# Running log-sum-exp over time: three rows per partition, the exponent written over the input, later rows added in PSUM by VectorE

## The chip, the cores and the metric

The kernel runs on one core of a Trainium2 chip. A core has TensorE (PE, matrix products into the PSUM memory), VectorE (DVE), ScalarE (ACT, here for Exp and Ln), GpSimd (POOL), and SyncE (SP), which here issues every transfer between the device memory and the on-chip memory (SBUF). Sixteen DMA engines carry the transfers out. The engines run side by side, each takes its own instructions in order, and they wait for each other by semaphores. The metric is the device time of one execution in microseconds (us), as the median of nine runs.

## What is computed

```python
def reference(x):                      # x: 4 x 4096 x 4128, float32
    out[:, 0, :] = x[:, 0, :].copy()
    for t in range(1, S):
        mx = np.maximum(out[:, t - 1, :], x[:, t, :])
        out[:, t, :] = mx + np.log(np.exp(out[:, t - 1, :] - mx) + np.exp(x[:, t, :] - mx))
```

For each of 4 batches and 4128 columns this is the logarithm of the running sum of exp(x) over 4096 time steps. Input and output are 270.5 MB each.

## The kernel before

A batch is cut in steps of 256 consecutive time steps, 16 steps to a batch, 64 in all. In a step each of 128 partitions holds R = 2 consecutive time steps of all 4128 columns, so that a partition's part of the transfer is one run of 33,024 bytes. One load (L102) brings the step into the tile `xt`; one store (L153) takes it out from the same tile after the results have been written over the input.

The columns are cut in four chunks of 1024 (`CH`), and the last chunk also has a tail of 32. For a chunk, ScalarE writes Exp of both rows as fp16 into a buffer of its own, `et` (L111). TensorE then sums over the partitions with triangular 0/1 matrices: `incl` times the first row adds, for partition p, the first rows of partitions 0 to p; `excl` times the second row adds the second rows of partitions 0 to p-1; `pick` times the carry adds what all earlier steps of the batch came to. All go into one PSUM tile `pt` (L86), which then holds the sums for the first row. ScalarE takes Ln of it into `xt` (L126). After that, two more matmuls with the identity `ident` add the second row, and a second Ln writes the second row of the result. The tail has a small PSUM tile of its own, `qt`, with both rows by matmuls, and one Ln (L149).

The carry is the last partition's sum after the last row. VectorE copies 32 partitions of `pt` to fp16 (L90) and writes what the copy lost as a second fp16 value (L91), two instructions of 1024 columns for each chunk (the function `keep`). The next step's `pick` adds both.

The order of the work is written out by hand, and each engine's queue follows it. Within a step, the method `run` starts a chunk's Exp and first matmuls (`head`) before the Lns of the chunk before it. There are five `xt` buffers, four `et` buffers, three `pt` tiles of two PSUM banks and two `qt` tiles. Loads are issued three steps ahead: before the work of step i comes the load of step i+3, after it the store of step i. Both go to SP's one queue, so a load that waits for its buffer holds the store behind it.

Of the kernel before, what the change touches and what calls it, by code (L numbers as in the profile page):

```python
# [7 lines left out]
FP32 = mybir.dt.float32  # L8
FP16 = mybir.dt.float16
ACT = mybir.ActivationFunctionType  # L10
P = 128
R = 2
CH = 1024
MM = 512
HI, LO = 96, 32


def _constants(nc, pool):


    def tri(base, name):
        t = pool.tile([P, P], FP16, name=name)
        nc.gpsimd.memset(t, 1.0)

        nc.gpsimd.affine_select(
            out=t, in_=t, pattern=[[1, P]], compare_op=mybir.AluOpType.is_ge,
            fill=0.0, base=base, channel_multiplier=-1,
        )
        return t

    def ones_where_zero(bases, step, name):
        t = pool.tile([P, P], FP16, name=name)
        nc.gpsimd.memset(t, 0.0)
        for base in bases:
            nc.gpsimd.affine_select(  # L35
                out=t, in_=t, pattern=[[step, P]], compare_op=mybir.AluOpType.not_equal,
                fill=1.0, base=base, channel_multiplier=1,
            )
        return t

    return (
        tri(0, "incl"),
        tri(-1, "excl"),
        ones_where_zero([0], -1, "ident"),
        ones_where_zero([-(HI + 31), -(LO + 31)], 0, "pick"),
    )


@with_exitstack
def kernel(  # L50
    ctx: ExitStack,
    tc: tile.TileContext,
    x: bass.AP,
    out: bass.AP,
):

    nc = tc.nc
    B, S, D = x.shape  # L60
    rows = P * R
    n_t = S // rows
    assert S % rows == 0
    n_main = D // CH
    tail = D - n_main * CH
    t0 = n_main * CH

    nc.scalar.preload_act_table_set("natural_log_exp_and_others")  # L68
    consts = ctx.enter_context(tc.tile_pool(name="consts", bufs=1))
    incl, excl, ident, pick = _constants(nc, consts)  # L70

    xpool = ctx.enter_context(tc.tile_pool(name="xpool", bufs=5))
    epool = ctx.enter_context(tc.tile_pool(name="epool", bufs=4))
    cpool = ctx.enter_context(tc.tile_pool(name="cpool", bufs=1))
    pmain = ctx.enter_context(tc.tile_pool(name="pmain", bufs=3, space=bass.MemoryType.PSUM))
    ptail = ctx.enter_context(tc.tile_pool(name="ptail", bufs=2, space=bass.MemoryType.PSUM))

    carry = [cpool.tile([P, CH], FP16, name=f"carry{c}") for c in range(n_main)]
    carry_t = cpool.tile([P, tail], FP16, name="carry_t")
    for t in (*carry, carry_t):  # L80
        nc.vector.memset(t, 0.0)  # L81

    ctx.enter_context(tc.manual_schedule())

    def mm(pt, w, rhs, start, stop):
        nc.tensor.matmul(pt, lhsT=w, rhs=rhs, start=start, stop=stop, skip_group_check=True)  # L86

    def keep(cr, pt):

        nc.vector.tensor_copy(cr[HI:HI + 32, :], pt[HI:HI + 32])  # L90
        nc.vector.tensor_tensor(  # L91
            out=cr[LO:LO + 32, :], in0=pt[HI:HI + 32], in1=cr[HI:HI + 32, :],
            op=mybir.AluOpType.subtract,
        )

    class Step:
        def __init__(self, b, k):
            self.first = k == 0
            self.xt = xpool.tile([P, R, D], FP32, name="xt")
            self.et, self.pt = {}, {}  # L100
            self.dram = lambda t: t[b, k * rows:(k + 1) * rows, :].rearrange("(p j) d -> p j d", j=R)
            nc.sync.dma_start(out=self.xt, in_=self.dram(x))  # L102

        def cols(self, c):
            return slice(c * CH, (c + 1) * CH if c + 1 < n_main else D)

        def exp(self, c):
            s = self.cols(c)
            w = s.stop - s.start
            et = epool.tile([P, R, CH + tail], FP16, name="et")  # L110
            nc.scalar.activation(et[:, :, :w], self.xt[:, :, s], ACT.Exp)  # L111
            self.et[c] = et

        def head(self, c):
            et = self.et[c]
            pt = self.pt[c] = pmain.tile([P, CH], FP32, name="pt")
            for s in range(0, CH, MM):
                mm(pt[:, s:s + MM], incl, et[:, 0, s:s + MM], True, False)
            for s in range(0, CH, MM):
                mm(pt[:, s:s + MM], excl, et[:, 1, s:s + MM], False, self.first)  # L120
            if not self.first:
                for s in range(0, CH, MM):
                    mm(pt[:, s:s + MM], pick, carry[c][:, s:s + MM], False, True)

        def ln(self, j, c):
            nc.scalar.activation(self.xt[:, j, c * CH:(c + 1) * CH], self.pt[c], ACT.Ln)  # L126

        def second(self, c):
            pt = self.pt[c]
            for s in range(0, CH, MM):  # L130
                mm(pt[:, s:s + MM], ident, self.et[c][:, 1, s:s + MM], False, True)

        def close(self, c):

            self.ln(1, c)
            keep(carry[c], self.pt[c])

        def tail_mm(self):
            et = self.et[n_main - 1]
            qt = self.qt = ptail.tile([P, R, tail], FP32, name="qt")  # L140
            e0, e1 = et[:, 0, CH:], et[:, 1, CH:]
            for j in range(R):
                mm(qt[:, j, :], incl, e0, j == 0, False)
                mm(qt[:, j, :], incl if j else excl, e1, False, self.first)
                if not self.first:
                    mm(qt[:, j, :], pick, carry_t, False, True)

        def ln_tail(self):
            nc.scalar.activation(self.xt[:, :, t0:D], self.qt, ACT.Ln)  # L149
            keep(carry_t, self.qt[:, 1, :])  # L150

        def store(self):
            nc.sync.dma_start(out=self.dram(out), in_=self.xt)  # L153

        def run(self):
            last = n_main - 1
            self.exp(0)
            self.head(0)
            for c in range(1, n_main):
                self.exp(c)  # L160
                self.head(c)
                if c == last:
                    self.tail_mm()
                self.ln(0, c - 1)
                self.second(c - 1)
                if c >= 2:
                    self.close(c - 2)
            self.ln(0, last)
            self.second(last)
            self.close(last - 1)  # L170
            self.ln_tail()
            self.close(last)
            self.store()

    work = [(b, k) for b in range(B) for k in range(n_t)]
    ahead = 3
    steps = []
    for i, (b, k) in enumerate(work):
        if i == 0:
            steps += [Step(*work[n]) for n in range(ahead)]  # L180
        if i + ahead < len(work):
            n = i + ahead
            steps.append(Step(*work[n]))
        steps[i].run()


# [28 lines left out]
```

The softmax here doesn't subtract the row's maximum and nothing guards it: scores larger than these inputs give would overflow.

## Time and profile before

| what | value |
|---|---|
| median of nine runs | 1265.33 us (1264.34 to 1266.58) |
| the profiled execution: time | 1265.88 us |
| the profiled execution: span from first to last instruction | 1264.1 us |
| busy: ScalarE, TensorE (matmuls), VectorE | 962.7, 665.7, 655.7 us |
| mean granted TensorE clock | 0.764 of full |
| transfers | 64 loads and 64 stores of 4128 KB each |
| from issue to landing, median: loads, stores | 29.4, 38.9 us |
| moved over the span | 541.51 MB, 428 GB/s |

An engine's busy time is the sum of its instructions, and says little about what the end waits for: ScalarE is busy for 76% of the span and is still not what the others wait for most of the time. For that one reads the waits of each engine, and for the transfers the forty slices of the span, in each of which the page gives the share that the DMA engines were busy in tenths, and the GB/s that they moved. A group's line has the engine, the operation, what it writes and reads, the count, then the busy sum and the mean in ns of one, then the idle time just before and what ended it.

### The profile page before, as it was taken

The page shows a single profiled execution, that of the slowest core. Times are in us where ns is not written, and L with a number is a line of the kernel's source. Part 1 is how long each engine was busy: PE and PEld are TensorE (multiplying, and loading weights), DVE is VectorE, ACT ScalarE, POOL GpSimd, SP SyncE. Part 2 cuts the span into 40 slices and gives each one's busy share as a digit, 9 for nine tenths or more (in the row PEclk, how much of TensorE's full clock was granted, in tenths as well). Part 3 has the DMA queues.
Part 4 walks back from the last instruction along what each step waited for, and adds up shares of the span by engine and source line. Part 5 has one row for each costly group of instructions (what it writes and reads, how often), then busy time and mean ns, then how long its engine had stood idle before and what let it go on. Part 6 is the DMA issues. An engine that isn't in the chain of part 4 may idle for free.

```text
span 1264.1 us, 7025 instructions
## 1 busy us (share of the span) xinstructions
PE 665.7 (53%) x2392; PEld 242.8 (19%) x2392; DVE 655.7 (52%) x645; ACT 962.7 (76%) x833; POOL 2.2 (0%) x13
## 2 busy tenths in 40 slices
PE   2666655545455464454554555556545555555551
PEld 1222221212111121121111211112111121112210
DVE  3665654464554645545546455464554544645443
ACT  5988877778677777787877777777778787787872
POOL 0000000000000000000000000000000000000000
PEclk9777777777777777877877777767777777777876
DMA  9999999999999999999999999999999999999997
GB/s 401 420 429 432 433 431 429 430 432 432 431 433 432 433 434 434 434 433 430 434 432 432 432 433 432 434 434 433 433 429 435 433 433 431 431 434 433 434 434 318
DMA packets 18466, 541.51 MB, mean 428 GB/s; under 512 B 2048, under 2 KB 2048, under 8 KB 2048
## 3 DMA queue, kind: packets, MB, share of 16 engines
q1 hardware_dynamic: 18432, 541.07, 99.4%
q8 instruction: 19, 0.31, 0.1%
q14 instruction: 15, 0.12, 0.0%
HBM read 270.53 MB, written 270.53 MB: 428 GB/s over the span
## 4 chain that ended last, share of the span: by engine, by line
DMA 84%; ACT 2%; issue 1%; SPq 1%; DVE 1%; PE 0%; ACTq 0%
DMA out_dram<-xt 80%; DMA xt<-in_x_dram 5%; ACT et L111 1%; ACT xt L126 1%; SPq L102 1%; PE pt L86 0%; DVE carry L90 0%; DVE carry L91 0%; SPq L153 0%; DVE carry_t L90 0%; DVE carry_t L91 0%; ACTq L126 0%
## 5 line engine op out<-in xcount | busy, mean ns | idle before, releaser
L90 DVE CAST carry<-pt 32x1024 f16<-32x1024 f32 x256 | 314.8, 1230 | 576.3 <-ACT xt L126 573.1
L111 ACT ACTIVATE et<-xt 128x2048 f16<-128x2048 f32 (+1 forms) x256 | 485.4, 1920 | 151.9 <-DMA xt<-in_x_dram 151.9
L126 ACT ACTIVATE xt<-pt 128x1024 f32<-128x1024 f32 x512 | 504.5, 1028 | 126.3 <-PE pt L86 65.7
L86 PE MATMUL pt<-et,incl 128*128 128x512 f16 x512 | 211.8, 506 | 548.2 <-ACT et L111 376.5
L91 DVE TENSOR_TENSOR carry<-pt,carry 32x1024 f16<-32x1024 f32 x256 | 314.0, 1227 | 8.8
L86 PE MATMUL pt<-et,excl 128*128 128x512 f16 x512 | 211.9, 506 | 0.0
L86 PEld LDWEIGHTS <-incl 128*128 128x128 f16 x704 | 69.3, 111 | 683.8 <-issue 635.1
L86 PE MATMUL pt<-carry,pick 128*128 128x512 f16 x480 | 195.2, 498 | 0.0
L86 PE MATMUL pt<-et,ident 128*128 128x512 f16 x512 | 175.4, 429 | 26.5 <-ACT xt L126 26.5
L86 PEld LDWEIGHTS <-excl 128*128 128x128 f16 x576 | 71.4, 124 | 116.8 <-issue 85.0
L86 PEld LDWEIGHTS <-pick 128*128 128x128 f16 x600 | 69.5, 118 | 95.1 <-issue 67.2
L86 PEld LDWEIGHTS <-ident 128*128 128x128 f16 x512 | 49.6, 106 | 101.3 <-issue 75.1
L86 PE MATMUL qt<-et,incl 128*128 128x32 f16 x192 | 19.8, 190 | 0.0
L86 PE MATMUL qt<-carry_t,pick 128*128 128x32 f16 x120 | 15.6, 182 | 0.0
L149 ACT ACTIVATE xt<-qt 128x64 f32<-128x64 f32 x64 | 14.5, 227 | 0.0
L90 DVE CAST carry_t<-qt 32x32 f16<-32x32 f32 x64 | 12.6, 197 | 2.0
L91 DVE TENSOR_TENSOR carry_t<-qt,carry_t 32x32 f16<-32x32 f32 x64 | 12.4, 193 | 2.2
L86 PE MATMUL qt<-et,excl 128*128 128x32 f16 x64 | 11.7, 183 | 0.0
L81 DVE MEMSET carry<- 128x512 uint32 x4 | 1.9, 485 | 1.1 <-PEq L199 1.0
L68 ACT ACT_TABLE_LOAD x1 | 1.3, 1283 | 0.8 <-PEq L199 0.8
L35 POOL TENSOR_SCALAR_AFFINE_SELECT pick<-pick 128x128 f16<-128x128 f16 x2 | 0.6, 297 | 0.1
L35 POOL TENSOR_SCALAR_AFFINE_SELECT ident<-ident 128x128 f16<-128x128 f16 x1 | 0.3, 298 | 0.0
(11 smaller groups left out, 1.9 us busy)
## 6 DMA issues: line engine op xcount, KB each, us to landing
xt<-in_x_dram SPq DMA_DIRECT2D x64, 4128.0 KB, 29.4
out_dram<-xt SPq DMA_DIRECT2D x64, 4128.0 KB, 38.9
```

What stands on the lines that cost most here:

```text
L35: nc.gpsimd.affine_select(out=t, in_=t, pattern=[[step, P]], compare_op=mybir.AluOpType.not_equal, fill=1.0, base=base, channel_multiplier=1,)
L68: nc.scalar.preload_act_table_set("natural_log_exp_and_others")
L81: nc.vector.memset(t, 0.0)
L86: nc.tensor.matmul(pt, lhsT=w, rhs=rhs, start=start, stop=stop, skip_group_check=True)
L90: nc.vector.tensor_copy(cr[HI:HI + 32, :], pt[HI:HI + 32])
L91: nc.vector.tensor_tensor(out=cr[LO:LO + 32, :], in0=pt[HI:HI + 32], in1=cr[HI:HI + 32, :], op=mybir.AluOpType.subtract,)
L102: nc.sync.dma_start(out=self.xt, in_=self.dram(x))
L111: nc.scalar.activation(et[:, :, :w], self.xt[:, :, s], ACT.Exp)
L126: nc.scalar.activation(self.xt[:, j, c * CH:(c + 1) * CH], self.pt[c], ACT.Ln)
L149: nc.scalar.activation(self.xt[:, :, t0:D], self.qt, ACT.Ln)
```

## The change

A partition now holds R = 3 consecutive time steps, one run of 49,536 bytes. 4096 is 32 times 128 rows, so a batch has ten steps of three rows and one of two; the two-row step is the last of a batch, and in the first batch the first. There are 44 steps. The `xt` buffers become four of 49.5 KB per partition. Exp is written as fp16 over the first half of the bytes that its chunk of `xt` had, in each row, and the `et` buffers are gone.

A chunk's `head` now puts only the first row's sums into `pt`: `incl` for the first row, `excl` for the second and third, and `pick`. After Ln has read `pt`, VectorE adds the next row's exponents to `pt` in place (`next_row`), and a further Ln follows, and so again for the third row. The identity matrix and its matmuls are gone. In the tail, the second and third row are made by VectorE adds too.

The order in a step runs over g, with the Lns of up to three chunks at different rows in each g. The keeps of chunks that are finished come ahead of the adds as long as a head of this step is still to come, and after the adds and after the last of the step otherwise. SP's order is now store n, then load n+3, both issued after the last Ln of step n.

The core of the diff, the rest of it being the removed class methods and the calls that go with them:

```diff
-R = 2
+R = 3
-    xpool = ctx.enter_context(tc.tile_pool(name="xpool", bufs=5))
-    epool = ctx.enter_context(tc.tile_pool(name="epool", bufs=4))
+    bufs = 4
+    xpool = ctx.enter_context(tc.tile_pool(name="xpool", bufs=bufs))
...
+    def add(o, a, v):
+        nc.vector.tensor_tensor(out=o, in0=a, in1=v, op=mybir.AluOpType.add)
...
-        def exp(self, c):
-            s = self.cols(c)
-            w = s.stop - s.start
-            et = epool.tile([P, R, CH + tail], FP16, name="et")
-            nc.scalar.activation(et[:, :, :w], self.xt[:, :, s], ACT.Exp)
-            self.et[c] = et
...
-        def second(self, c):
-            pt = self.pt[c]
-            for s in range(0, CH, MM):
-                mm(pt[:, s:s + MM], ident, self.et[c][:, 1, s:s + MM], False, True)
...
+        def load(self):
+            full = xpool.tile([P, R, D], FP32, name="xt")
+            self.xt = full[:, :self.r, :]
+            self.half = self.xt.bitcast(FP16)
             nc.sync.dma_start(out=self.xt, in_=self.dram(x))
...
+        def e(self, j, a, b):
+            return self.t.half[:, j, 2 * self.c * CH + a:2 * self.c * CH + b]
+
+        def exp(self):
+            c0, w = self.c * CH, self.w
+            nc.scalar.activation(
+                self.t.half[:, :, 2 * c0:2 * c0 + w], self.t.xt[:, :, c0:c0 + w], ACT.Exp,
+            )
+
+        def head(self):
+            t = self.t
+            pt = self.pt = pmain.tile([P, CH], FP32, name="pt")
+            for j in range(t.r):
+                for s in range(0, CH, MM):
+                    mm(pt[:, s:s + MM], excl if j else incl, self.e(j, s, s + MM), start=j == 0)
+            if not t.first:
+                for s in range(0, CH, MM):
+                    mm(pt[:, s:s + MM], pick, carry[self.c][:, s:s + MM])
+            if self.c == last:
+                self.tail_head()
+
+        def tail_head(self):
+            t, r = self.t, self.t.r
+            full = ptail.tile([P, R, tail], FP32, name="qt")
+            qt = self.qt = full[:, :r, :]
+            e = [self.e(i, CH, CH + tail) for i in range(r)]
+            for i in range(r):
+                mm(qt[:, 0, :], excl if i else incl, e[i], start=i == 0)
+            if not t.first:
+                mm(qt[:, 0, :], pick, carry_t)
+            for i in range(1, r):
+                add(qt[:, i, :], qt[:, i - 1, :], e[i])
+
+        def stage(self, j):
+            t, c = self.t, self.c
+            nc.scalar.activation(t.xt[:, j, c * CH:(c + 1) * CH], self.pt, ACT.Ln)
+            if c == last and j == 0:
+                nc.scalar.activation(t.xt[:, :, t0:D], self.qt, ACT.Ln)
+
+        def next_row(self, j):
+            add(self.pt, self.pt, self.e(j + 1, 0, CH))
...
+    for n, s in enumerate(steps):
+        chunks = [Chunk(s, c) for c in range(n_main)]
+        chunks[0].exp()
+        chunks[1].exp()
+        chunks[0].head()
+        done = []
+        for g in range(n_main + s.r - 1):
+            at = [(chunks[g - d], d) for d in range(s.r - 1, -1, -1) if 0 <= g - d < n_main]
+            for k, d in at:
+                k.stage(d)
+            if g == n_main + s.r - 2:
+                s.store()
+                if n + ahead < len(steps):
+                    steps[n + ahead].load()
+            done += [k for k, d in at if d + 1 == s.r]
+            if g + 1 < n_main:
+                while done:
+                    done.pop(0).keep()
+            for k, d in at:
+                if d + 1 < s.r:
+                    k.next_row(d)
+            if g + 2 < n_main:
+                chunks[g + 2].exp()
+            if g + 1 < n_main:
+                chunks[g + 1].head()
+        for k in done:
+            k.keep()
```

## The prediction

> **What bounds the kernel now.** I read the forty slices first, then the queues, the queue engine's own waits, its timeline, and last the groups of instructions.
>
> ```profile
> DMA  9999999999999999999999999999999999999997
> GB/s 401 420 429 432 433 431 429 430 432 432 431 433 432 433 434 434 434 433 430 434 432 432 432 433 432 434 434 433 433 429 435 433 433 431 431 434 433 434 434 318
> q1 hardware_dynamic: 18432, 541.07, 99.4%
> ```
>
> Every slice but the last has the DMA engines busy, at 429 to 435 GB/s from the third on. 99.4% of the 1264.1 us span, 1256.5 us, is packets of the loads and stores. The kernel is bound by its transfers, and the only slack is some 3 us in the first two slices and 8 us in the last.
>
> ```profile
> SPq L102 <- DMA out_dram<-xt: 1087.8, 59, 19.8
> SPq L153 <- ACT xt L126: 84.5, 7, 17.9
> 566.59 0.33 SPq L102 DMA_DIRECT2D xt<-in_x_dram  x1
> 567.01 0.38 SPq L153 DMA_DIRECT2D out_dram<-xt  x1
> 586.10 0.33 SPq L102 DMA_DIRECT2D xt<-in_x_dram  x1
> 605.60 0.33 SPq L102 DMA_DIRECT2D xt<-in_x_dram  x1
> ```
>
> The first two lines are SP's waits (total, count, longest): 59 of 64 loads wait for an older store to leave its buffer, and only 7 stores wait for ScalarE. The issues come every 19.5 us, and a store goes 0.42 us behind a load because it stood ready and was only queued after it. So a step of 2 rows (8.454 MB both ways) costs 19.5 us of DMA, and a step of 3 rows at this rate 29.3 us.
>
> ```profile
> 29.11 0.34 SPq L153 DMA_DIRECT2D out_dram<-xt  x1
> 45.29 0.34 SPq L153 DMA_DIRECT2D out_dram<-xt  x1
> 61.80 0.34 SPq L153 DMA_DIRECT2D out_dram<-xt  x1
> 78.30 0.34 SPq L153 DMA_DIRECT2D out_dram<-xt  x1
> ```
>
> Near the start the stores do wait for the compute, and show its own pace: 16.2, 16.5 and 16.5 us a step. The compute has 3 us to spare in 19.5. What this change does to that pace decides the case.
>
> ```profile
> L90 DVE CAST carry<-pt 32x1024 f16<-32x1024 f32 x256 | 314.8, 1230 | 576.3 <-ACT xt L126 573.1
> L111 ACT ACTIVATE et<-xt 128x2048 f16<-128x2048 f32 (+1 forms) x256 | 485.4, 1920 | 151.9 <-DMA xt<-in_x_dram 151.9
> L126 ACT ACTIVATE xt<-pt 128x1024 f32<-128x1024 f32 x512 | 504.5, 1028 | 126.3 <-PE pt L86 65.7
> L91 DVE TENSOR_TENSOR carry<-pt,carry 32x1024 f16<-32x1024 f32 x256 | 314.0, 1227 | 8.8
> 617.27 1.01 PE L86 MATMUL pt<-et,incl 128*128 128x512 f16 x2 [5.14 <-ACT et L111]
> 618.08 1.06 PE L86 MATMUL pt<-et,excl 128*128 128x512 f16 x2
> 603.44 0.59 PE L86 MATMUL pt<-et,incl 128*128 128x512 f16 x2 [0.64 <-ACT et L111]
> 603.87 0.59 PE L86 MATMUL pt<-et,excl 128*128 128x512 f16 x2
> ```
>
> These are the durations I use. The matmul pairs show two paces: after 5.14 us of idling a pair follows every 0.81 to 0.85 us, in a busy stretch every 0.43.
>
> **What the Trainium skill says.** "DMA: Bandwidth & Descriptors", Where 436 GB/s comes from: the SBUF ports cap the sixteen engines at about 435 GB/s. The slices agree, at 429 to 435, so longer runs have under 1% to win. The same page, How a descriptor splits into AXI transactions: a start off a 256-byte boundary costs extra beats. 33,024 bytes is 129 times 256, and 49,536 is 193.5 times, so every second partition's run would start off it. No trace here shows that; by the page it is 4 of some 1,550 beats. "VectorE: DVE Perf Modes", The perf-mode tier table: a tensor_tensor with a PSUM operand has only the slowest mode; L91's 1227 ns for 1024 elements agrees. "TensorE: Matmul & The Clock Gate", Part 1: after an idle window of about 3.4 us the array runs at half clock. The two paces above agree.
>
> **The change, part by part.** Loads and stores: 128 of 4128 KB become 80 of 6192 KB and 8 of 4128 KB, the same bytes. A 33 KB packet takes an engine 1256.5/1024 = 1.227 us; at 435 GB/s it would be 1.215. If that 12 ns is per packet, the 320 packets fewer per engine (1024 to 704) save at most 3.8 us; if the excess goes with the bytes, or half is lost to the unaligned starts, 0 to 2 us. I take 2.
>
> SP: before, load i+3 went ahead of store i. Now store n is queued first and load n+3 behind it, so a late compute also holds the load. In flight when store n-1 lands are load n+2, store n and then load n+3, each 14.7 us: 44 us of work, as deep as the 39 us that a store takes to land now. The loads land two steps early, so the order itself costs nothing while the compute keeps pace.
>
> The mask constant, the second matmuls (L86 with ident, 175.4 us of PE) and the separate exponent buffers go. PE is not on the path, so this gains nothing; but PE is now emptier and colder.
>
> New on VectorE: 336 adds of 128x1024 in PSUM (per 3-row step 8, per 2-row step 4). None is in the trace. L91 reads PSUM and SBUF and takes 1.227; I take 1.23 plus the 0.03 seen between VectorE instructions. At best 1.17; at worst, if reading and writing one PSUM bank halves the rate, 2.3. The keeps fall from 256 to 176, and carry_t's from 64 to 44. VectorE's sum is 336 x 1.23 + 176 x 2.46 + 44 x 0.39 + 84 x 0.2, some 880 us of the span. That is no bound by itself, but the add stands between two Lns of one chunk, where a matmul stood before.
>
> ScalarE: Ln goes from 1.028 at 1024 elements to 0.227 at 64, 0.834 ns per element; so an Exp of 3 x 1024 is 1.90 + 0.85 = 2.76, and of 3 x 1056 2.85. A step has 4 Exps, 12 Lns and a tail Ln of 0.25: 23.7 us of work for 29.3 us of DMA. Because Exp writes over x, an Exp and the Ln behind it wait for the end of the one before, which loses the 0.10 us by which neighbours overlap now.
>
> I lay a 3-row step out by hand, with time from Exp of chunk 0, a head of eight matmuls at half clock (8 x 0.43 + 0.16 = 3.6), and 0.03 to 0.1 us for each handover:
> - Exp 0 to 2.8, Exp 1 to 5.55. Head 0 runs 2.8 to 6.4, so Ln of chunk 0 (first row) ends at 7.5; one microsecond is lost to the cold head.
> - Exp 2 to 10.1, two Lns to 12.1, Exp 3 to 14.85, three Lns to 17.7. The adds lie beside the Exps.
> - The keep of chunk 0 is ahead of the adds here, since head 3 needs its PSUM buffer (three buffers, four chunks): VectorE 15.9 to 18.4, then adds of chunks 1 and 2 to 19.7 and 20.95. ScalarE idles from 17.7 to 19.7.
> - Ln chunk 1 (last row) to 20.7, Ln chunk 2 to 22.0. Head 3 runs 18.5 to 22.1, Ln chunk 3 to 23.1, tail Ln to 23.3.
> - Nothing covers the rest: adds of 2 and 3 to 24.55 and 25.8, Lns to 25.6 and 26.85, add to 28.1, last Ln to 29.2. The next Exp starts at 29.1, as neighbours overlap. The remaining keeps lie under the next step's two Exps.
>
> At full clock heads 0 and 3 are 1.7 us shorter each and the period is 27.9, the keep and adds setting the middle. Head 0 follows some 9 us of idle PE and head 3 some 5, so both should be cold: I take 29.0. A 2-row step laid out so comes to 22 against 19.5 of DMA.
>
> The sum on the compute: first load landed at 13.1 (as now), 21 for the first 2-row step, 40 x 29.0, 3 x 22, and 11 for the last store: 1271 us of span. The sum on the DMA: 1264.1 less 2, 1262. The longer one sets the end. The profiled run took 1265.88 with its span 1264.1, and the median of nine is 1265.33, so 1.2 goes on top: **1272 us**.
>
> **The rivals.** A, the compute chain takes the bound, as worked out: 1266 to 1292 for a period of 28.85 to 29.5, likeliest 1272. For it: ScalarE's idle stretches are all dependencies. Against it: its margin over the DMA is 9 us in 1271, 0.25 us a step.
>
> B, on the other side: the DMA keeps the bound and only the packet saving is seen. It decides where the period is under (1262 - 13.1 - 21 - 66 - 11)/40 = 28.8. For it: PEclk 0.76 in the trace, so heads are not always cold, and 27.9 at full clock. Then 1261 to 1262.7, faster, if most of the 12 ns is per packet (1264.1 - 3.8 + 1.2 at best); 1263 to 1265.3, no change, if it isn't.
>
> C, one cost is mis-taken in the large: an add at 2.3 us puts five times 1.07 us on the chain, 40 x 5.3 = 214, near 1485; an add of 1.30 only 14 us, 1286; unaligned runs that cost more than the page's beats come to 12 us for each per cent.
>
> That the change does not do what it says: the bytes are fixed and the runs are contiguous per partition, so they will be 49.5 KB; I give it nothing.
>
> **How the numbers follow.** A 0.60, B faster 0.16, B unchanged 0.16, C 0.08. A measurement of this kernel tells about 0.2%, 2.5 us, from no change. Of A, 0.04 falls within that, so slower is 0.64, same 0.20, faster 0.16. The range takes in B, with 1 us below its best, from 1260, and A with an add or handover somewhat dearer, to 1292; beyond lies most of C. A's own range is 1266 to 1292.
>
> **What would show it.** Right: SP's stores waiting for ScalarE's Ln in most steps at a period of 28.8 to 29.5, DMA slices below 9 or GB/s under 430 late in the run, ScalarE idle behind VectorE's adds, PEclk below 0.76. Wrong: loads still waiting for old stores all along and a cadence of 29.3 with ScalarE waiting for loads (B), or an add far from 1.23 us (C).

## The result and the profile after

The changed kernel takes 1273.48 us (median of nine runs, 1272.98 to 1274.32). The ratio to the kernel before, measured beside it, is 1.0063, with a 95% interval of 1.0055 to 1.0071: 8 us slower. The profiled execution has a span of 1272.1 us against 1264.1.

The slices of the changed kernel (busy tenths, granted clock in tenths, GB/s; each slice is 31.8 us):

```profile
PEclk8666676767667667676666767676666767676666
DMA  9999999999999999999999999999999999999977
GB/s 407 427 429 426 431 435 429 438 429 434 431 436 432 427 438 430 430 441 432 428 434 436 429 435 435 430 439 426 434 435 437 429 435 433 434 435 430 431 312 307
```

The transfers are still full until the last two slices. What is new is there: two slices at 312 and 307 GB/s where the kernel before had one at 318. The DMA engines have work as long as loads run ahead, and when the last load is in they can only wait for stores that come at the pace of the compute. PEclk has gone from 0.764 to 0.674.

SP's waits and its last issues in the changed kernel say who is late:

```profile
SPq L117 <- ACT xt L160: 1201.7, 44, 28.5
SPq L114 <- DMA out_dram<-xt: 6.9, 6, 2.5
1150.64 0.34 SPq L117 DMA_DIRECT2D out_dram<-xt  x1
1179.64 0.34 SPq L117 DMA_DIRECT2D out_dram<-xt  x1
1208.76 51.74 SPq L117 DMA_DIRECT2D out_dram<-xt  x3
```

All 44 stores wait for ScalarE's last Ln, 1201.7 us in total, where before 59 loads had waited 1087.8 us for old stores. Now six loads do, for 6.9 us. The stores come 29.0 to 29.1 us apart, and the last three are spread over 51.7 us because the steps behind them are still being computed.

The chain of waits that ended last (shares of the span by engine), then the waits of ScalarE for a load and for VectorE's adds, and those of the adds for the tail's Ln (L162):

```profile
ACT 48%; DVE 25%; PE 21%; issue 4%; DMA 1%; ACTq 0%
ACT xt L129 <- DMA xt<-in_x_dram: 10.9, 1, 10.9
ACT xt L160 <- DVE pt L89: 217.2, 175, 2.9
DVE pt L89 <- ACT xt L162: 35.9, 44, 2.0
```

Before, 84% of this chain was DMA; now 1% is. ScalarE waits for a load once, for the first. From there to the last Ln the compute is one unbroken chain, in which ScalarE waits 175 times for one of VectorE's adds.

The groups whose durations the prediction had worked out without having seen them:

```profile
L89 DVE TENSOR_TENSOR pt<-pt,xt 128x1024 f32<-128x1024 f32 x336 | 402.0, 1229 | 220.3 <-ACT xt L160 182.7
L129 ACT ACTIVATE xt<-xt 128x3072 f16<-128x3072 f32 x120 | 330.9, 2757 | 1.3
L129 ACT ACTIVATE xt<-xt 128x3168 f16<-128x3168 f32 x40 | 113.8, 2845 | 0.0
```

An add in place in PSUM takes 1229 ns (1.23 us was taken), an Exp of 3 x 1024 2757 ns (2.76) and one of 3 x 1056 takes 2845 (2.85).

One step of three rows on ScalarE, from the timeline of the changed kernel (start, duration, count, idle before and who ended it; some lines in between are left out):

```profile
584.13 5.55 ACT L129 ACTIVATE xt<-xt 128x3072 f16<-128x3072 f32 x2
590.54 1.02 ACT L160 ACTIVATE xt<-pt 128x1024 f32<-128x1024 f32 x1 [0.87 <-PE pt L86]
598.95 2.85 ACT L160 ACTIVATE xt<-pt 128x1024 f32<-128x1024 f32 x3
603.80 3.28 ACT L160 ACTIVATE xt<-pt 128x1024 f32<-128x1024 f32 x3 [1.99 <-DVE pt L89]
608.52 1.02 ACT L160 ACTIVATE xt<-pt 128x1024 f32<-128x1024 f32 x1 [1.30 <-DVE pt L89]
612.09 1.02 ACT L160 ACTIVATE xt<-pt 128x1024 f32<-128x1024 f32 x1 [1.36 <-DVE pt L89]
613.01 1.90 ACT L129 ACTIVATE xt<-xt 128x2048 f16<-128x2048 f32 x1
```

Count from 584.13: the cold head costs 0.87 us before 6.4, the keep of chunk 0 and the add behind it 1.99 before 19.7, and the two idle stretches at the end 1.30 and 1.36. The next step's Exp starts at 28.9.

TensorE and VectorE around the fourth head of the same step:

```profile
602.64 1.01 PE L86 MATMUL pt<-xt,incl 128*128 128x512 f16 x2 [6.49 <-DVE carry L94]
606.16 0.43 DVE L89 TENSOR_TENSOR qt<-qt,xt 128x32 f32<-128x32 f32 x2 [1.27 <-PE qt L86]
607.25 2.36 DVE L89 TENSOR_TENSOR pt<-pt,xt 128x1024 f32<-128x1024 f32 x2 [0.66 <-ACT xt L162]
```

The head is cold: after 6.49 us without work its first pair of matmuls takes 1.01 us, where a pair in a busy stretch took 0.59. The tail's two adds stand next in VectorE's queue and wait for it until 606.16. The adds of chunks 2 and 3 come behind them, and then wait 0.66 us more for the tail's Ln, though the Ln of chunk 2 that comes before its add had ended at 605.95.

### The profile page after: what moved, and what is told of

It is laid out like the page before. It is cut to its first block, busy times and chain, and to the rows that moved or that the text cites. A ratio compares the mean times of both kernels' runs of the same rounds, so it can differ in the third digit from the quotient of the medians.

```text
span 1272.1 us, 5283 instructions
## 1 busy us (share of the span) xinstructions
PE 479.5 (38%) x1512; PEld 178.7 (14%) x1512; DVE 869.8 (68%) x865; ACT 978.4 (77%) x733; POOL 1.8 (0%) x11
## 3 DMA queue, kind: packets, MB, share of 16 engines
q1 hardware_dynamic: 12672, 541.07, 98.6%
## 4 chain that ended last, share of the span: by engine, by line
ACT 48%; DVE 25%; PE 21%; issue 4%; DMA 1%; ACTq 0%
ACT xt L129 27%; ACT xt L160 21%; PE pt L86 20%; DVE pt L89 14%; DVE carry L93 6%; DVE carry L94 6%; DMA xt<-in_x_dram 1%; ACT xt L162 1%; PE qt L86 0%; ACTq L160 0%; DVE carry_t L93 0%; DVE carry_t L94 0%
## 5 line engine op out<-in xcount | busy, mean ns | idle before, releaser
L89 DVE TENSOR_TENSOR pt<-pt,xt 128x1024 f32<-128x1024 f32 x336 | 402.0, 1229 | 220.3 <-ACT xt L160 182.7
L129 ACT ACTIVATE xt<-xt 128x3072 f16<-128x3072 f32 (+3 forms) x176 | 475.4, 2701 | 12.3 <-DMA xt<-in_x_dram 10.9
L86 PE MATMUL pt<-xt,incl 128*128 128x512 f16 x352 | 155.1, 536 | 772.2 <-ACT xt L129 501.1
L93 DVE CAST carry<-pt 32x1024 f16<-32x1024 f32 x176 | 216.5, 1230 | 107.5 <-ACT xt L160 103.5
L86 PE MATMUL pt<-xt,excl 128*128 128x512 f16 x672 | 261.4, 528 | 0.0
L94 DVE TENSOR_TENSOR carry<-pt,carry 32x1024 f16<-32x1024 f32 x176 | 215.9, 1227 | 6.1
L86 PEld LDWEIGHTS <-incl 128*128 128x128 f16 x396 | 43.0, 116 | 847.9 <-issue 841.4
L86 PE MATMUL pt<-carry,pick 128*128 128x512 f16 x320 | 129.8, 497 | 0.0
L86 PEld LDWEIGHTS <-excl 128*128 128x128 f16 x756 | 94.7, 129 | 159.8 <-issue 131.9
L86 PEld LDWEIGHTS <-pick 128*128 128x128 f16 x360 | 44.1, 122 | 65.3 <-issue 48.1
L162 ACT ACTIVATE xt<-qt 128x96 f32<-128x96 f32 (+1 forms) x44 | 10.7, 244 | 0.0
## 6 DMA issues: line engine op xcount, KB each, us to landing
xt<-in_x_dram SPq DMA_DIRECT2D x40, 6192.0 KB, 40.6
```

Of the source, the lines that this page charges most:

```text
L86: nc.tensor.matmul(pt, lhsT=w, rhs=rhs, start=start, stop=False, skip_group_check=True)
L89: nc.vector.tensor_tensor(out=o, in0=a, in1=v, op=mybir.AluOpType.add)
L94: nc.vector.tensor_tensor(out=cr[LO:LO + 32, :], in0=pt[HI:HI + 32], in1=cr[HI:HI + 32, :], op=mybir.AluOpType.subtract,)
L129: nc.scalar.activation(self.t.half[:, :, 2 * c0:2 * c0 + w], self.t.xt[:, :, c0:c0 + w], ACT.Exp,)
L162: nc.scalar.activation(t.xt[:, :, t0:D], self.qt, ACT.Ln)
```

## The experiments

Each is an edit to the changed kernel unless it says otherwise, and ratios are to the kernel before, measured beside it.

**A third of the stores.** The edit:

```diff
-            nc.sync.dma_start(out=self.dram(out), in_=self.xt)
+            nc.sync.dma_start(out=self.dram(out)[:, :1, :], in_=self.xt[:, :1, :])
```

> The changed kernel with only the first row of each partition stored, so two thirds of the output are left out; the computation and its order stay. Bytes fall from 541 to some 363 MB, which at 433 GB/s is 840 us of transfers. If the compute chain is the bound (A), the period of a 3-row step stays 29.1 us and the time falls only by the shorter last store, to 1264 to 1270 us. If the transfers bind (B), it falls to 850 to 1000 us.

Measured: 1267.1 us, ratio 1.0014 (1.0007 to 1.0021), with 363.5 MB moved instead of 541.1.

```profile
DMA  9987777766677777766687777764679777766412
SPq L117 <- ACT xt L162: 1206.6, 44, 28.5
```

With a third of the traffic gone, the packets of the loads and stores take 69.5% of the span in place of 98.6%, and the time falls by only 6.4 us. All of that lies in the last store, which carries less and, as it needs only the first row and the tail, goes out 2.5 us earlier: the last Ln ends at 1260.06 us, against 1260.14 with all stores. The chain of compute is the bound.

**The transfers alone, two rows and three.** All computation is left out in both: in the kernel before `steps[i].run()` becomes `steps[i].store()`, in the changed one the loop over a step's chunks becomes

```diff
+        s.store()
+        if n + ahead < len(steps):
+            steps[n + ahead].load()
```

> The kernel before with all computation left out: each step is loaded and stored again, two rows per partition, runs of 33,024 bytes. If the kernel before is bound by its transfers, 1256 to 1266 us. If part of its time is compute, clearly less, under 1250.

> The changed kernel with all computation left out: loads and stores of three rows per partition, runs of 49,536 bytes, in the changed kernel's order on SP. If the 12 ns of excess is per packet, 2 to 4 us below the two-row copy; if it goes with the bytes, the same within 1.5 us; if the starts off a 256-byte boundary cost more than a few beats, above it by 5 us or more. It also gives the time that the changed kernel would have if its compute were free.

Measured: 1261.05 us for two rows (ratio 0.9968, 0.9955 to 0.998) and 1258.66 for three (0.9944, 0.9931 to 0.9956). The runs of the two copies do not overlap (1260.43 to 1263.91 and 1258.21 to 1258.78). So the three-row transfers are 2.4 us faster, no more, with whatever the starts off a 256-byte boundary cost already in it. The copies also differ in the number of buffers and in the order on SP, and no run takes these apart from the longer runs. The kernel before stands 4.4 us above its own transfers.

**The tail later.** Same operations, another order:

```diff
-            if c == last and j == 0:
+            if c == last and j == t.r - 1:
                 nc.scalar.activation(t.xt[:, :, t0:D], self.qt, ACT.Ln)
...
-            for i in range(1, r):
-                add(qt[:, i, :], qt[:, i - 1, :], e[i])
+            self.et = e
...
         def next_row(self, j):
+            if self.c == last and j == 0:
+                for i in range(1, self.t.r):
+                    add(self.qt[:, i, :], self.qt[:, i - 1, :], self.et[i])
             add(self.pt, self.pt, self.e(j + 1, 0, CH))
```

> The changed kernel with the tail's adds moved behind the add of chunk 2 and the tail's Ln moved to the end of the step; the same operations. In the trace of the changed kernel the adds of chunks 2 and 3 wait for the tail's Ln. A: that wait is on the chain, the period falls from 29.1 to 28.3 to 28.6 us, the chain's sum 13 + 21 + 40 x 28.45 + 66 + 11 = 1249 falls under the transfers and the time is that of the transfers, 1260 to 1266 us. Rival: the tail's wait is covered by the adds behind it, and the time stays at 1271 to 1275 us.

Measured: 1263.91 us, ratio 0.9986 (0.9979 to 0.9993). SP's stores and waits, near the start and in total:

```profile
62.00 0.34 SPq L117 DMA_DIRECT2D out_dram<-xt  x1
90.08 0.34 SPq L117 DMA_DIRECT2D out_dram<-xt  x1
118.17 0.34 SPq L117 DMA_DIRECT2D out_dram<-xt  x1
SPq L114 <- DMA out_dram<-xt: 401.6, 33, 18.6
```

The free period, the pace of the compute where no load holds it up, is 28.1 us, a little under the 28.3 to 28.6 that were expected and against 29.1 in the same stretch of the changed kernel, and 33 loads wait for old stores again. One microsecond a step turns the bound back to the transfers and cuts the time by 9.6 us. The edit moves both the tail's adds and its Ln of 96 elements out of the way of the add of chunk 2. In the step shown above the wait for that Ln alone was 0.66 us; how the microsecond divides between the two no run shows. This version beats both kernels, the kernel before by 0.14%.

**A warm array.** Matmuls into a spare PSUM bank that nobody reads (to make room, the tail's PSUM tiles go from two to one):

```diff
                 chunks[g + 1].head()
+                for i in range({2: 14, 3: 34}.get(g + 1, 0)):
+                    mm(fill, incl, zeros, start=i == 0)
```

> The changed kernel with matmuls added that nobody reads: 14 of 128x512 after the third head of each step and 34 after the fourth, into a PSUM bank of their own (the tail's tiles go from two to one), so that TensorE does not idle. A: the cold heads 0 and 3 are on the chain; with PEclk above 0.85 the period falls to 28.0 to 28.5 us and the time to that of the transfers, 1260 to 1266 us. Rival: the heads are covered by the Exps and the keep, and the time stays at 1271 to 1276 us.

Measured: 1268.19 us, ratio 1.0023 (1.0014 to 1.0032), clock 0.887. From the first store at 34.01 us to the ninth at 259.62 the period is 28.2 us, against 29.1 in the changed kernel: warming the array is worth 0.9 us a step, as expected, and loads wait for old stores again (33 times, 371.2 us). Not every head was warm. In the step of 27.7 us behind the store at 203.93 the first pair of the first head takes 0.59 us; in the one of 28.9 us behind the store at 118.29 it comes after 3.64 us of idle array and takes 1.01. But the transfers end later than in the run before, and the time missed its window by 2 us.

**Both edits,** with 30 added matmuls behind the fourth head.

> The added matmuls (14 and 30 a step) and the later tail together. Both theories of the two runs before it predict the transfers as the bound with more to spare: a free period of 27.9 us, the time 1260 to 1264 us, which is the three-row copy's time within 0.3%, and loads that wait for old stores again on SP. If it stays above 1268 us the bound is neither the tail's wait nor the cold array.

Measured: 1267.57 us, ratio 1.0018 (1.001 to 1.0025). The free period is 27.2 us (33.95 to 251.47 over eight steps; 27.9 was expected), and SP waits for old stores for 501.8 us. So the transfers are the bound, with more to spare than in the run with the later tail alone, and yet the time is 3.7 us longer. The expectation missed: the floor, the time that the transfers need, had itself risen, which the last experiment bears out. On the queue of fetched instructions this run has more packets:

```profile
q8 instruction: 27, 0.44, 0.1%
```

The changed kernel and the run with the later tail have 12 such packets, the copies none.

**Keeps always first.**

```diff
-            if g + 1 < n_main:
-                while done:
-                    done.pop(0).keep()
+            while done:
+                done.pop(0).keep()
```

> The changed kernel with a chunk's keep always ahead of the adds, also when no head of the step is left. A: VectorE is on the chain at the end of the step; the keep of chunk 1 (2.5 us) goes ahead of the adds of chunks 2 and 3, and that of chunk 2 partly ahead of the last add, so the period rises by 3 to 5 us to 32 to 34 and the time to 1385 to 1470 us. Rival: VectorE is idle for a third of the span and takes it up; 1273 us as before.

Measured: 1409.08 us, ratio 1.1136 (1.1116 to 1.1157); the period is 32.4 us. VectorE's stretch at the end of a step in this run:

```profile
607.51 1.23 DVE L93 CAST carry<-pt 32x1024 f16<-32x1024 f32 x1
608.78 1.23 DVE L94 TENSOR_TENSOR carry<-pt,carry 32x1024 f16<-32x1024 f32 x1
610.04 2.36 DVE L89 TENSOR_TENSOR pt<-pt,xt 128x1024 f32<-128x1024 f32 x2
612.43 1.23 DVE L93 CAST carry<-pt 32x1024 f16<-32x1024 f32 x1
613.70 1.23 DVE L94 TENSOR_TENSOR carry<-pt,carry 32x1024 f16<-32x1024 f32 x1
614.96 1.23 DVE L89 TENSOR_TENSOR pt<-pt,xt 128x1024 f32<-128x1024 f32 x1
```

The two keeps stand in front of the adds, so that ScalarE waits 3.19 us for the add behind the first keep and 2.76 us for the one behind the second, where the changed kernel has waits of 1.30 and 1.36. The part of the change that puts the adds first is worth 3.4 us a step; without it the change would have cost 11%.

**The old order on SP,** load n+3 ahead of the work of step n:

```diff
+        if n + ahead < len(steps):
+            steps[n + ahead].load()
         chunks = [Chunk(s, c) for c in range(n_main)]
...
                 s.store()
-                if n + ahead < len(steps):
-                    steps[n + ahead].load()
```

> The changed kernel with the old order on SP: load n+3 is issued ahead of the work of step n, its store behind it. The load must wait for store n-1, which was issued just before and takes 27 us to land, and store n then waits behind the load. If the order on SP is free (as the prediction had it), 1271 to 1276 us. If four buffers do not allow the old order, stores come late and the DMA runs dry: 1290 to 1330 us.

Measured: 1430.44 us, ratio 1.1305 (1.1284 to 1.1326); in the right direction, but 157 us above the changed kernel where 17 to 57 were expected.

```profile
572.81 0.33 SPq L114 DMA_DIRECT2D xt<-in_x_dram  x1
573.23 0.38 SPq L117 DMA_DIRECT2D out_dram<-xt  x1
606.59 0.33 SPq L114 DMA_DIRECT2D xt<-in_x_dram  x1
571.00:573.00 2.00, 0.00 (x0) 0.00 (x0) 0.69 (x1) 1.97 (x2) 0.00 (x0) 0.88 0.00 0
```

A load waits for the store that was issued right behind the load before it, so only this one pair is ever in flight. It takes 33.8 us, and the DMA engines stand empty before the next pair comes (the last line is the stretch from 571 to 573 us, with a DMA share of 0.00 and 0 GB/s). The expectation had named the dry DMA engines and put their cost far too low. With four buffers the new order on SP is needed.

**The copy with TensorE's instructions,** to find why the runs with added matmuls were slower at the same bound. The three-row copy and, in each step,

```diff
+        for i in range(80):
+            mm(fill, incl, zeros, start=i == 0)
         s.store()
```

> The three-row copy again (all computation left out) with 80 matmuls a step that read constants and that nobody reads, 3520 in all, so TensorE's instruction stream is as long as in the run with both edits; no engine touches the loaded data and no transfer waits for TensorE. The profile lists packets of instructions fetched on queue q8: 12 in the changed kernel and in the later-tail run, 27 and 29 in the runs with added matmuls, none in the copies, and the spans rise with them. If fetching TensorE's instructions takes time from the DMA engines, q8 shows some 27 packets and the time rises by 5 to 12 us over the three-row copy, to 1264 to 1271 us. If the runs with added matmuls were slow for another reason (waits, the one tail tile, traffic of the engines), it stays at 1258 to 1261 us.

Measured: 1263.83 us, ratio 0.9988 (0.9981 to 0.9994), with 27 packets on q8. That is 5.2 us above the same copy without them, 0.19 us for each packet, at the low end of the 5 to 12 us that were expected. Stores in the copy without matmuls (first two lines) and in this run (last two):

```profile
749.22 0.43 SPq L117 DMA_DIRECT2D out_dram<-xt  x1
1061.57 0.34 SPq L117 DMA_DIRECT2D out_dram<-xt  x1
753.29 0.43 SPq L120 DMA_DIRECT2D out_dram<-xt  x1
1065.82 0.34 SPq L120 DMA_DIRECT2D out_dram<-xt  x1
```

The matmuls end at 765 us. Up to there this run falls behind by 4.1 us, and in the next 300 us by hardly more (4.25 at 1065.82); the step after that adds 0.7 us for which no cause is known. No engine touches the data here and SP waits only for transfers, so matmuls in the stream, with the fetching of their instructions, cost a run that is bound by its transfers this time. Whether the fetching does it or the matmuls' running, no run separates. For the fetching speaks that its packets are carried beside the others (the profile counts them in the same 16 engines' time), and that the delay does not grow evenly: it is 1.0 us at 321 and at 438 us alike, while the matmuls run on. Against it speaks an estimate: at the copy's 431 GB/s, 0.44 MB takes 1.0 us, so their bytes alone are not enough.

## Why the prediction was right

- **The bound moves to the compute (rival A): right, and shown.** With a third of the stores gone the time fell by 6.4 us; with one microsecond of waiting taken out of the step it fell by 9.6.
- **The sum: right within 1 us of span, part of it by errors that cancel.** The first store goes out at 33.91 us (13.1 and 21 were taken). The 40 three-row steps take 28.96 us on average (1226.2 us from the first store's issue to the last Ln's end at 1260.14, less the two-row steps, over 40), the two-row steps 22.46, 22.74 and 22.45, the end 12; 1272.1 together, where the sum said 1271. The median is 1273.5, where the forecast was 1272. The average of the long steps hides two kinds: 37 of them take 29.06, and the three that come first in a batch, whose heads have no carry to add, only 27.82. The sum had not told them apart. That saved 3.5 us against its 29.0, and the two-row steps, the end and the other long steps took 4.7 us more than it gave them.
- **The layout of the step.** The first Ln of chunk 0, which the layout has end at 7.5, starts at 6.41 and ends at 7.43; the idle stretch from 17.7 to 19.7 is 1.99 long in the trace; the last Ln was put to end at 29.2 and ends at 29.0. Both heads behind an idle array were cold (9.73 and 6.49 us without work, 9 and 5 in the layout). Warming the array gave 0.9 us a step, where the layout's gap between 29.1 and 27.9 said 1.2; of single steps in that run the shortest took 27.7 us, and one with a cold first head 28.9.
- **The adds on the path.** Taken at L91's 1.23 us, found at 1.229 in place. The bound of 2.3 us, a bank read and written at half rate, did not occur.
- **The keeps.** The layout put them under the next step's Exps. Where they were moved ahead of the adds, the period rose by 3.4 us.
- **The order on SP costs nothing: right for the new order,** since after the first load ScalarE never waited for one. That the loads land two steps early is wrong: a load is issued two steps, some 58 us, ahead of its use and takes 40.6 us to land (median), which leaves 17 us, less than one step. The old order, not the new, is the one that four buffers cannot afford.
- **The packet saving: 2 us taken, 2.4 measured** between the copies, which differ in buffers and order too. Rival B's premise was sound, and its place, transfers as the bound, exists: it is the run with the later tail, 1263.9 us, beside the 1263 of B's floor. The changed kernel missed that place by the margin that the prediction named, a quarter of a microsecond a step. With a margin so small the direction could have gone the other way, as the prediction's own odds say.
- **What was missed is inside the layout:** it had the adds of chunks 2 and 3 follow the tail's Ln, and took that for the order of things. The Ln writes other columns than the add of chunk 2 reads, and the tail's adds and Ln could be moved. And the floor of the transfers was taken as fixed, when matmuls in the stream move it by several us.

## What to carry to other kernels

A kernel bound by its transfers gains only what the transfers give back, and that can be measured alone by leaving the computation out; here the three-row transfers had 2.4 us of 1261 to give. When such a change lengthens the compute's own period, lay one step out instruction by instruction against the transfers' period: busy sums (ScalarE 23.7 us of 29.3 here) do not show that dependencies make it 29. Where the two periods meet, look for short instructions that sit between long ones: here the place of the tail's two adds (0.43 us) and its Ln (0.24 us) decided the sign.

## What was not expected

Matmuls that touch none of the data take time from transfers, by their running or by the fetching of their instructions: 3520 of them cost a pure copy 5.2 us, with 27 packets of 0.44 MB in all on the instruction queue, and the two runs that warmed the array ended some 4 us later than the run with the later tail, though in all three the loads waited for old stores again. What warming the array gained in the compute, it lost in part in the transfers.
